# An encoder block's front stage: conditioning, normalization and first projections put in another order

## The chip, the cores and the metric

One core of a Trainium2 chip (trn2). The time is microseconds of device time for one execution of the program; the kernel before was run three times, and the profile is of one execution of its own.

## What is computed

One layer of an encoder, for two sequences of 512 tokens with 1024 channels and one conditioning vector each; all in fp32. Cut to what matters here:

```python
mod = silu(c) @ w_ada + b_ada                       # 1024 -> 6 x 1024
sh1, sc1, gt1, sh2, sc2, gt2 = split(mod, 6)
h = rmsnorm(x, g_attn) * (1 + sc1) + sh1
z = h @ w_in                                        # 1184 columns here, 2048 of gates later
qa, ka, va, cq, ckv, kr, gla, glb = split(z)
# mixer A: windowed attention on rope(rmsnorm(qa)), rope(rmsnorm(ka)), va
# mixer B: rmsnorm(cq) @ w_uq, rmsnorm(ckv) @ w_ukv, norm, rope, dense attention
x = x + gt1 * ((sigmoid(gla) * (oa @ w_o_a) + sigmoid(glb) * (ob @ w_o_b)) @ w_out)
# then an MLP with a depthwise convolution, modulated by sh2, sc2, gt2
```

A projection in fp32 accuracy is three matmuls of fp32r halves (`mm3`: high x high, high x low, low x high), so each weight and each activation is first split into a high part (a cast) and a low part (the residual).

## The kernel before

The front stage, which the change rebuilds, runs in this order (lines are those of the profile):

- **Constants.** Small loads on SP's queue: `colt`, `gcol` twice, `c_in`, `bcol` (L59 to L139). The Silu of c gives `c_s`.
- **Normalization of the first sequence.** `norm(t)` (L243) loads 128 tokens of x, squares them on ACT in two halves (L249), forms 1/rms by a Sqrt and a Newton step on VectorE (`rsqrt`, L83) and scales the tile on VectorE (L254).
- **First loop**, eight turns k (L269). Each loads 1 MB of the weights of sh1 and sc1 (`w_ada`, three buffers, L271), multiplies (64 small matmuls, L281), copies the row (L286), transposes the first sequence's block k of x (L104) and the row (L289), runs the first projection (`project`, 416 columns: cq, ckv, kr) for the block before, completes `mod` and `a1` (L295, L297), and makes the block's h: ACT scales and shifts (L112), VectorE casts (L113) and forms the residual (L114). In turns 3 to 6 stands `norm` of the second sequence's tiles; in turn 7 the rope tables are loaded and multiplied with the gains on VectorE (`tables`, L190; `table`, L171). The projection's weights are split on POOL (`split_pool`, L69 and L72).
- **Second sequence's h**, eight blocks (L301), with the low-rank weights w_uq and w_ukv loaded into the `w_ada` buffers and split by ACT and VectorE in between (`low_rank`, L218, L230, L231).
- **Low-rank stage** (mixer B), `prep_b` (L340) for eight tiles of 128 tokens in three steps that overlap; for the second sequence `z_tile` (L329) makes the tile's projection first. Its results go to DRAM on SP's queue (L403).
- **Mixer A**, two parts of 384 columns: `weights(1)`, `weights(2)` load and split (L201, ACT casts L210, residuals L212 on POOL, some on VectorE in part 2), then eight tiles each of `z_tile` and `prep_a` (L405). Between the tiles stands one step of `ada()` (L141): the conditioning's second half, two parts of eight steps, each a 1 MB load and four matmul groups of 512 columns (L151); after each part VectorE adds the bias (L155), TensorE transposes (L158), VectorE copies to `mod`.

Behind it come the gates' products (L491, weights split on POOL), which fill TensorE during attention, then attention, the output projection and the MLP.

What sets the order: each engine runs its instructions in the order of one list, which a scheduler forms from the program; it may put a later instruction first where an earlier one isn't ready by its own model of times. Instructions marked `keep_in_program_order` stay in place. All DMAs are issued from SP's queue, in order; a store that waits for its data holds the loads behind it. Tiles of a pool share a number of buffers (`bufs`), handed out in program order.

## Time and profile before

| | |
|---|---|
| three runs, median (lowest, highest) | 1456.73 us (1453.19, 1458.41) |
| profiled execution, its own time | 1456.77 us |
| its span, first to last instruction | 1455.0 us |
| granted clock of TensorE, mean | 0.992 |
| DMA, mean over the span | 133 GB/s |

A row of the timeline is a merged group of like instructions. "Idle before" is the time in which the engine did nothing just ahead of the instruction, with what ended it. PE is TensorE, DVE VectorE, ACT ScalarE, POOL GpSimd; SPq is the queue that issues DMAs. In a table by stage the numbers of an engine are busy microseconds and, in brackets, instructions; PEclk is the granted clock of TensorE, 1.00 being full speed; the DMA share is that of 16 engines' time.

### The profile page before, as it was taken

The numbers are of one execution on the slowest core, as the hardware profiler recorded it, in microseconds if no ns is written. First come the engines' busy times: TensorE is split into PE (matmuls) and PEld (weight loads), VectorE is DVE, ScalarE is ACT, GpSimd is POOL, SyncE is SP. The second block draws the span as 40 slices with busy tenths as digits, with TensorE's granted clock in tenths as the row PEclk, the third lists the DMA queues.
The fourth block names the chain that finished last, engine by engine and source line by source line (L and its number), as shares of the span: only waits on it lengthen the run. The fifth ranks groups of instructions, "written<-read, shape, count | busy, mean of one in ns | idle before, by whom it ended". The sixth has DMA issues, their size and how long they took to land.

```text
span 1455.0 us, 20795 instructions
## 1 busy us (share of the span) xinstructions
PE 1391.8 (96%) x7184; PEld 1153.1 (79%) x7184; DVE 1000.3 (69%) x1907; ACT 679.3 (47%) x1385; POOL 596.0 (41%) x592
## 2 busy tenths in 40 slices
PE   5888998999999999999998899999999999999998
PEld 4777776888888888878887767888888888888887
DVE  5788776666678886545479888777777787447433
ACT  3475223666666665422347455555555554212210
POOL 3174023442433442381005755555555545544430
PEclk9999999999999999999999999999999999999999
DMA  8565763322222213655312322222222327646522
GB/s 342 176 216 170 236 239 135 116 88 87 88 87 73 102 64 120 236 176 200 133 39 73 120 74 87 87 82 85 87 85 82 102 73 250 205 148 223 180 87 73
DMA packets 107801, 193.82 MB, mean 133 GB/s; under 512 B 18856, under 2 KB 39592, under 8 KB 104624
## 3 DMA queue, kind: packets, MB, share of 16 engines
q1 hardware_dynamic: 107696, 192.49, 39.8%
q8 instruction: 57, 0.93, 0.3%
q14 instruction: 48, 0.39, 0.1%
HBM read 148.39 MB, written 44.06 MB: 132 GB/s over the span
## 4 chain that ended last, share of the span: by engine, by line
PE 77%; DVE 13%; POOL 3%; ACT 2%; DMA 2%; issue 2%; SPq 0%; ACTq 0%; POOLq 0%; DVEq 0%
PE px L955 13%; PE psg L491 11%; PE py L955 7%; PE psd L79 5%; PE psd L80 5%; PE psd L81 5%; PE pz L955 3%; PE ppt L512 3%; PE ppo L575 2%; PE psx L81 2%; PE psx L80 2%; PE psx L79 2%; PE psz L79 2%; PE psy L81 1%; PE psy L79 1%
## 5 line engine op out<-in xcount | busy, mean ns | idle before, releaser
L955 PE MATMUL px<-t,wt 128*128 128x512 f32 x792 | 191.2, 391 | 7.0 <-ACT tmp_cc L960 6.3
L922 POOL TENSOR_TENSOR wt<-wraw,wt 128x512 fp32r<-128x512 f32 x66 | 92.8, 1410 | 232.2 <-ACT wt L921 232.0
L955 PEld LDWEIGHTS px<-t,wt 128*128 128x128 f32 x792 | 148.0, 188 | 41.1 <-ACT tmp_cc L960 9.5
L491 PE MATMUL psg<-h_hi,wg 128*128 128x512 f32 x512 | 170.2, 397 | 0.0
L506 POOL TENSOR_SCALAR p<-p,l 128x512 f32<-128x512 f32 (+2 forms) x128 | 78.8, 617 | 200.3 <-DVE l L505 125.7
L76 DVE TENSOR_TENSOR wd<-wraw,wd 128x512 fp32r<-128x512 f32 x88 | 93.1, 1098 | 96.4 <-ACT wd L75 96.4
L79 PE MATMUL psd<-wd 128*128 128x512 f32 x352 | 136.9, 389 | 0.0
L80 PE MATMUL psd<-wd 128*128 128x512 f32 x352 | 136.9, 389 | 0.0
L81 PE MATMUL psd<-wd 128*128 128x512 f32 x352 | 136.9, 389 | 0.0
L75 ACT CAST wd<-wraw 128x512 fp32r<-128x512 f32 x88 | 51.3, 620 | 156.1 <-issue 86.9
L491 PEld LDWEIGHTS psg<-h_hi,wg 128*128 128x128 f32 x512 | 95.9, 189 | 18.4 <-POOL wg L69 0.8
L491 PE MATMUL psg<-h_lo,wg 128*128 128x512 f32 x256 | 101.8, 397 | 0.0
L504 ACT ACTIVATE p<-pps,nm 128x512 f32<-128x512 f32 (+2 forms) x128 | 78.2, 611 | 39.3 <-DVE nm L501 31.7
L922 DVE TENSOR_TENSOR wt<-tmp_sf,wt 128x512 fp32r<-128x512 f32 x88 | 82.2, 944 | 12.2 <-ACT wt L921 12.0
L967 DVE SCALAR_TENSOR_TENSOR tmp_u<-tmp_cc,cw,tmp_u 128x511 f32<-128x511 f32 x66 | 64.3, 974 | 37.3 <-ACT tmp_u L966 37.2
L69 POOL TENSOR_SCALAR wd<-wraw 128x512 fp32r<-128x512 f32 x44 | 34.2, 777 | 112.0 <-PE psd L81 63.9
L81 PEld LDWEIGHTS psd<-wd 128*128 128x128 f32 x352 | 66.1, 188 | 13.8
L79 PEld LDWEIGHTS psd<-wd 128*128 128x128 f32 x352 | 66.1, 188 | 13.7
L80 PEld LDWEIGHTS psd<-wd 128*128 128x128 f32 x352 | 66.1, 188 | 13.6
L501 DVE TENSOR_REDUCE nm<-pps 128x1 f32<-128x512 f32 (+2 forms) x128 | 74.7, 584 | 3.1 <-PE pps L81 1.5
L966 ACT ACTIVATE tmp_u<-tmp_cc,cw 128x512 f32<-128x512 f32 x66 | 53.6, 813 | 45.7 <-DMA g_d<-tmp_u 25.6
L72 POOL TENSOR_TENSOR wd<-wraw,wd 128x512 fp32r<-128x512 f32 x44 | 72.7, 1653 | 3.7
(257 smaller groups left out, 3517.8 us busy)
## 6 DMA issues: line engine op xcount, KB each, us to landing
w_ada<-in_w_ada_dram SPq DMA_DIRECT2D x24, 1024.0 KB, 7.1
wraw<-in_w_up_dram SPq DMA_DIRECT2D x96, 256.0 KB, 2.7
wraw<-in_w_down_dram SPq DMA_DIRECT2D x88, 256.0 KB, 3.6
g_d<-tmp_u SPq DMA_DIRECT2D x44, 256.0 KB, 2.4
wraw<-g_d SPq DMA_DIRECT2D x44, 256.0 KB, 2.7
wg_raw<-in_w_g_dram SPq DMA_DIRECT2D x16, 512.0 KB, 3.7
gate_d<-go SPq DMA_DIRECT2D x32, 256.0 KB, 2.0
ldb<-qb_d SPq DMA_DIRECT2D x8, 1024.0 KB, 4.9
```

Of the source, the lines that this page charges most:

```text
L72: G.tensor_sub(lo, raw, hi.bitcast(F32))
L76: V.tensor_sub(lo, raw, hi.bitcast(F32))
L79: PE.matmul(ps, lhsT=lh, rhs=rh, start=first, stop=False)
L80: PE.matmul(ps, lhsT=lh, rhs=rl, start=False, stop=False)
L81: PE.matmul(ps, lhsT=ll, rhs=rh, start=False, stop=last)
L491: PE.matmul(ps, lhsT=w[:, wl, m, k, :], rhs=hl[b][:, k, :], start=k == 0 and n == 0, stop=k == KD - 1 and n == 2)
L501: V.tensor_reduce(nm, ps[:, :n], op=ALU.max, axis=AX.X, negate=True)
L504: A.activation(p[:, :n], ps[:, :n], AF.Exp, bias=nm, accum_out=l)
L506: G.tensor_scalar(out=p[:, :plen], in0=p[:, :plen], scalar1=l, scalar2=1.0, op0=ALU.mult, op1=ALU.mult)
L922: lo_eng.tensor_sub(w[:, 1], raw, w[:, 0].bitcast(F32))
L955: PE.matmul(ps[:, sl], lhsT=w[:, wl, i], rhs=h[:, hl, sl], start=not add and i == 0 and n == 0, stop=i == 3 and n == 2, skip_group_check=add)
L967: V.scalar_tensor_tensor(out=u[:, 1:S], in0=src[:, 0:S - 1], scalar=cw[:, cc, 0:1], in1=u[:, 1:S], op0=ALU.mult, op1=ALU.add)
```

## The change

- The two `gcol` loads move behind the second sequence's h; `colt` and `bcol` behind the four loads of x.
- Normalization: tiles in pairs. One square of 1024 elements a tile (written to `h_lo[1]` or `h_hi[1]`, which are not in use yet), one root for two tiles; tile 3 is scaled on ACT. The second sequence's tiles are loaded in turns 2 to 5 and squared on ACT in the same turns; in turn 5 one root for all four, scaled on ACT. A Sqrt of a constant stands ahead of it all.
- Sixty transposes of the identity on TensorE ahead of the first turn; their result isn't used.
- In the first loop the projection of the block before is cut in two, on both sides of the row's transpose. The second sequence's first block is made in turn 7.
- The rope tables stand after the loop, behind the loads of the first two low-rank weights, and are multiplied on POOL.
- `ada()` loads two steps ahead, from the end of the second sequence's h on. Its steps stand in the low-rank stage: three a tile in the first four tiles, then one a tile; none in mixer A.
- `weights_late` loads the weights of mixer A in two pieces of four blocks into the `w_ada` buffers; part 1 is split at the end of the low-rank stage, part 2 ahead of the last `prep_a` of part 1; residuals go to POOL and VectorE in turn.

```diff
@@ table
-            V.tensor_mul(tc_, tc_, bcast(g, 1, [128, NT, dim]))
+            G.tensor_mul(tc_, tc_, bcast(g, 1, [128, NT, dim]))
...
@@ ada
+            ws = []
+
+            def load():
+                n = len(ws)
+                if n < 2 * KD:
+                    w = zp.tile([128, KD, 4, 64], F32, name="w_ada", bufs=3).rearrange("p a b c -> p (a b c)")
+                    SY.dma_start(w, w_ada[n // KD, n % KD])
+                    ws.append(w)
+
+            load()
+            load()
+            yield
             for part in range(2):
...
                 for k in range(KD):
-                    w = zp.tile([128, KD, 4, 64], F32, name="w_ada", bufs=3).rearrange("p a b c -> p (a b c)")
-                    SY.dma_start(w, w_ada[part, k])
+                    load()
+                    w = ws[part * KD + k]
@@ new
+        def weights_late(part):
+            c0, cw = ZC[part]
+            raws = []
+            for k in range(0, KD, 4):
+                raw = zp.tile([128, KD, 4, 64], F32, name="w_ada", bufs=3).rearrange("p a b c -> p (a b c)")[:, :4 * cw]
+                raw = raw.rearrange("p (k n) -> p k n", k=4)
+                SY.dma_start(raw, w_z[:, k:k + 4, c0:c0 + cw])
+                raws.append(raw)
+
+            def split():
+                tiles = []
+                for k in range(KD):
+                    w, raw = zp.tile([128, 2, ZB], F32R, name="wz", bufs=10), raws[k // 4][:, k % 4]
+                    A.copy(w[:, 0, :cw], raw)
+                    (V if k % 2 else G).tensor_sub(w[:, 1, :cw], raw, w[:, 0, :cw].bitcast(F32))
+                    tiles.append(w)
+                return tiles
+            return split
@@ normalization of the first sequence
+            for t in range(NT):
+                load_x(t)
+            SY.dma_start(colt, cols)
+            SY.dma_start(bcol, b_col)
+            one = wk.tile([128, 1], F32, name="one")
+            V.memset(one, 1.0)
+            tc.keep_in_program_order(A.activation(one, one, AF.Sqrt))
+            for t in range(0, NT, 2):
+                ss = wk.tile([128, 2], F32, name="ss", bufs=2)
+                for j in range(2):
+                    xt = xn[t + j].rearrange("p (a n) -> p a n", a=2)
+                    A.activation(h_lo[1][:, 2 * (t + j):2 * (t + j) + 2, :], xt, AF.Square, accum_out=ss[:, j:j + 1])
+                r = scales(ss)
+                V.tensor_scalar(out=xn[t], in0=xn[t], scalar1=r[:, 0:1], scalar2=None, op0=ALU.mult)
+                if t:
+                    A.activation(xn[t + 1], xn[t + 1], AF.Copy, scale=r[:, 1:2])
+                else:
+                    V.tensor_scalar(out=xn[t + 1], in0=xn[t + 1], scalar1=r[:, 1:2], scalar2=None, op0=ALU.mult)
+
+            idle = pst.tile([128, S], F32, name="pst")
+            for j in range(60):
+                PE.transpose(idle[:, (j % NT) * 128:(j % NT + 1) * 128], ident, ident)
@@ first loop
-                if 3 <= k < 7:
-                    norm(NT + k - 3)
-                if k == 7:
-                    tables()
+                if 2 <= k < 6:
+                    load_x(NT + k - 2)
...
-                xt = transposed(pst, xn[:NT], k, True)
+                xt = transposed(pst, xf[:NT], k, True)
+                if k:
+                    project(k - 1, 0, 2)
                 pt = psa.tile([64, 128], F32, name="psa")
                 tc.keep_in_program_order(PE.transpose(pt, row, ident))
                 if k:
-                    project(k - 1)
+                    project(k - 1, 2, NT)
...
                 modulated(wk, xt, 0, a1, 0, h_hi[0], h_lo[0], k)
-            project(KD - 1)
-            for k in range(KD):
-                split = low_rank(k // 2) if k % 2 == 0 else split
-                modulated(wk, transposed(pst, xn[NT:], k), 1, a1, 0, h_hi[1], h_lo[1], k)
-                if k % 2:
-                    split()
+                if 2 <= k < 6:
+                    t = NT + k - 2
+                    A.activation(h_hi[1][:, 2 * (k - 2):2 * (k - 1), :], xn[t].rearrange("p (a n) -> p a n", a=2), AF.Square,
+                                 accum_out=ss1[:, k - 2:k - 1])
+                if k == 5:
+                    r1 = scales(ss1)
+                    for t in range(NT):
+                        A.activation(xn[NT + t], xn[NT + t], AF.Copy, scale=r1[:, t:t + 1])
+                if k == 7:
+                    second_batch()
+            project(KD - 1, 0, NT)
+            mods = ada()
+            splits = [low_rank(n) for n in range(2)]
+            tables()
+            for k in range(0, KD, 2):
+                if k == 4:
+                    splits += [low_rank(n) for n in range(2, 4)]
+                second_batch()
+                second_batch()
+                splits[k // 2]()
+            next(mods)
+            SY.dma_start(gcol[0:NOPE, 0:1], gains[2 * AD:2 * AD + NOPE].unsqueeze(1))
...
@@ low-rank stage and mixer A
             for t in range(2 * NT + 2):
+                for _ in range(3 if t < NT else 1):
+                    next(mods, None)
+                if t == 2 * NT - 1:
+                    later = weights_late(1)
...
+                if t == 2 * NT:
+                    tiles = later()
...
-            mods = ada()
+            later = weights_late(2)
             for part in range(2):
-                tiles = weights(1 + part)
                 for t in range(2 * NT):
-                    prep_a(t, z_tile(t, tiles, ZC[1 + part][1]), part)
-                    next(mods, None)
-            for _ in mods:
-                pass
+                    zt = z_tile(t, tiles, ZC[1 + part][1])
+                    if not part and t == 2 * NT - 1:
+                        tiles = later()
+                    prep_a(t, zt, part)
```

`scales` is the mean, the epsilon and `rsqrt` for all its columns; `second_batch` is one block of the second sequence's h, as before: four transposes and `modulated`.

## Rows read from the trace of the kernel before

**Rows 1.** The page, part 1: busy time of each engine, share of the span, instructions.
```profile
PE 1391.8 (96%) x7184; PEld 1153.1 (79%) x7184; DVE 1000.3 (69%) x1907; ACT 679.3 (47%) x1385; POOL 596.0 (41%) x592
```

**Rows 2.** Busy time of each engine by stage, the front in five stretches.
```profile
core 0: us, PE busy (x) PEld busy (x) DVE busy (x) ACT busy (x) POOL busy (x), PEclk, DMA share, GB/s
0.00:14.50 14.50, 0.00 (x0) 0.01 (x1) 3.75 (x22) 8.37 (x22) 0.96 (x7) 1.00 0.71 259
14.50:60.95 46.45, 38.69 (x655) 33.02 (x656) 30.97 (x102) 14.32 (x33) 14.01 (x16) 0.96 0.71 255
60.95:73.20 12.25, 11.10 (x65) 9.24 (x63) 11.71 (x23) 8.67 (x15) 2.62 (x2) 1.00 0.78 274
73.20:146.00 72.80, 63.44 (x330) 53.58 (x329) 61.87 (x179) 46.12 (x127) 44.52 (x79) 0.98 0.58 193
146.00:226.00 80.00, 73.50 (x429) 57.99 (x428) 62.03 (x212) 19.27 (x51) 18.94 (x19) 0.97 0.71 231
```

**Rows 3.** The same for the stretch in which the first loop loads.
```profile
14.00:40.00 26.00, 21.35 (x395) 18.30 (x395) 18.21 (x56) 7.84 (x20) 10.83 (x12) 1.00 1.02 400
```

**Rows 4.** The timeline of the first loop: start, duration, engine, line, operation, [idle before].
```profile
3.55 1.85 SPq L245 DMA_DIRECT2D xt<-in_x_dram  x4
14.52 1.94 PE L281 MATMUL pa<-w_ada,c_s 128*32 128x64 f32 x64 [14.52 <-DMA w_ada<-in_w_ada_dram]
17.84 1.52 DVE L254 TENSOR_SCALAR xt<-xt,r 128x1024 f32<-128x1024 f32 x1
29.76 1.10 PE L281 MATMUL pa<-w_ada,c_s 128*32 128x64 f32 x64
33.75 1.10 PE L281 MATMUL pa<-w_ada,c_s 128*32 128x64 f32 x64
33.87 2.71 POOL L72 TENSOR_TENSOR wz<-wz_raw,wz 128x416 fp32r<-128x416 f32 x2
34.91 0.33 SPq L271 DMA_DIRECT2D w_ada<-in_w_ada_dram  x1
54.70 1.10 PE L281 MATMUL pa<-w_ada,c_s 128*32 128x64 f32 x64
```

**Rows 5.** The chain of waits in the fifth turn: start, duration, what.
```profile
33.44 1.01 DVE xt L254
35.69 1.43 DVE h_lo L114
```

**Rows 6.** VectorE's groups by line, 14.5 to 73.2 us: busy us, mean ns, idle before.
```profile
L114 DVE TENSOR_TENSOR h_lo<-tmp,h_hi 128x512 fp32r<-128x512 f32 x16 | 12.5, 792 | 0.3
L113 DVE CAST h_hi<-tmp 128x512 fp32r<-128x512 f32 x16 | 7.5, 476 | 5.2 <-ACT tmp L112 5.2
L231 DVE TENSOR_TENSOR ukv<-w_ada,ukv 128x512 fp32r<-128x512 f32 x2 | 2.2, 1087 | 0.0
L231 DVE TENSOR_TENSOR uq<-w_ada,uq 128x768 fp32r<-128x768 f32 x2 | 1.9, 950 | 0.0
```

**Rows 7.** Durations of products on VectorE and POOL, ns min/median/max.
```profile
L177 DVE TENSOR_TENSOR tca<-tca,g_tab x2: 420/423/426, 60.4 to 62.8; 128x256 f32<-128x256 f32 x2
L324 POOL TENSOR_TENSOR t1b<-qf,tcb x8: 725/862/1510, 81.5 to 138.5; 128x256 f32<-128x256 f32 x8
L212 DVE TENSOR_TENSOR wz<-wz_raw,wz x4: 547/554/809, 116.3 to 175.8; 128x384 fp32r<-128x384 f32 x4
```

**Rows 8.** TensorE's conditioning matmuls, 73.2 to 226 us: busy us, mean ns, idle before.
```profile
L151 PE MATMUL psa<-w_ada,c_s 128*32 128x512 f32 x128 | 18.1, 604 | 0.0
```

**Rows 9.** DMA issues of the front: count, KB each, median us to landing.
```profile
w_ada<-in_w_ada_dram SPq DMA_DIRECT2D x24, 1024.0 KB, 7.1
```

**Rows 10.** The timeline where the front stage ends.
```profile
206.59 0.17 DVE L95 TENSOR_SCALAR rs<-rs 128x6 f32<-128x6 f32 x1
213.17 1.25 DVE L95 TENSOR_SCALAR rs<-rs 128x6 f32<-128x6 f32 x1
224.76 1.12 PE L158 MATMUL psa<-ident,br 128*128 128x128 f32 x4 [6.13 <-DVE br L155]
```

More of the change, by code (lines that the diff above doesn't have):

```diff
@@ L58, in encoder_block @@
     colt = const.tile([128, 16], F32, name="colt")
-    SY.dma_start(colt, cols)
     mod = const.tile([128, 48, NB], F32, name="mod")
@@ L64, in encoder_block @@
     V.memset(gcol, 1.0)
-    SY.dma_start(gcol[0:NOPE, 0:1], gains[2 * AD:2 * AD + NOPE].unsqueeze(1))
-    SY.dma_start(gcol[0:NOPE, 1:2], gains[2 * AD + BQK:2 * AD + BQK + NOPE].unsqueeze(1))
     def split_pool(hi, lo, raw, in_order=False):
@@ L241, in encoder_block, with load_x @@
             xn = [None] * (2 * NT)
-            def norm(t):
+            def load_x(t):
                 xt = wk.tile([128, D], F32, name="xt", bufs=2 * NT)
                 SY.dma_start(xt, x[t * 128:(t + 1) * 128, :])
-                ss = wk.tile([128, 2], F32, name="ss", bufs=4)
-                for q in range(2):
-                    junk = wk.tile([128, S], F32, name="tmp", bufs=2)
-                    A.activation(junk, xt[:, q * S:(q + 1) * S], AF.Square, accum_out=ss[:, q:q + 1])
-                r = wk.tile([128, 1], F32, name="r", bufs=4)
-                V.tensor_add(r, ss[:, 0:1], ss[:, 1:2])
-                mean_eps(r, r, D)
-                rsqrt(wk, r, 1)
-                V.tensor_scalar(out=xt, in0=xt, scalar1=r, scalar2=None, op0=ALU.mult)
-                xn[t] = lambda k, xt=xt: xt[:, k * 128:(k + 1) * 128]
@@ L257, in encoder_block, with scales, part_of @@
-            for t in range(NT):
-                norm(t)
+                xn[t] = xt
+            def scales(ss):
+                n = ss.shape[1]
+                r = wk.tile([128, 4], F32, name="r", bufs=3)[:, :n]
+                mean_eps(r, ss, D)
+                rsqrt(wk, r, n)
+                return r
+            def part_of(t):
+                return lambda k: xn[t][:, k * 128:(k + 1) * 128]
+            xf = [part_of(t) for t in range(2 * NT)]
+            for t in range(NT):
+                load_x(t)
@@ L261, in encoder_block, with project @@
             cw = ZC[0][1]
-            def project(k):
-                for t in range(NT):
+            def project(k, t0, t1):
+                for t in range(t0, t1):
                     sl = slice(t * 128, (t + 1) * 128)
@@ L267, in project, with second_batch @@
                         k == 0, k == KD - 1)
+            ss1 = wk.tile([128, NT], F32, name="ss1")
+            r1 = None
+            second = iter(range(KD))
+            def second_batch():
+                k = next(second, None)
+                if k is not None:
+                    modulated(wk, transposed(pst, xf[NT:], k), 1, a1, 0, h_hi[1], h_lo[1], k)
             for k in range(KD):
@@ L299, in encoder_block @@
                 modulated(wk, xt, 0, a1, 0, h_hi[0], h_lo[0], k)
-            project(KD - 1)
-            for k in range(KD):
-                split = low_rank(k // 2) if k % 2 == 0 else split
-                modulated(wk, transposed(pst, xn[NT:], k), 1, a1, 0, h_hi[1], h_lo[1], k)
-                if k % 2:
-                    split()
+                if 2 <= k < 6:
[20 more added lines that the diff above has]
+            SY.dma_start(gcol[0:NOPE, 0:1], gains[2 * AD:2 * AD + NOPE].unsqueeze(1))
+            SY.dma_start(gcol[0:NOPE, 1:2], gains[2 * AD + BQK:2 * AD + BQK + NOPE].unsqueeze(1))
             zfirst = []
```

5 lines of the change are left out of this document (2 added, 3 removed).

## The prediction

> **What bounds the kernel now.** The page comes first: over the span TensorE is busy 96% of the time, VectorE 69% [rows 1], so a gain must come from stretches where TensorE is held up. The table by stage shows where those are [rows 2]: nothing runs on TensorE for 14.5 us; in the next 46.45 us (first half of the conditioning, first projection) it is busy 38.69; then 11.10 of 12.25, 63.44 of 72.8 and 73.50 of 80. The column beside it names the partner: from 60.95 to 146 VectorE is busy 11.71 of 12.25 and 61.87 of 72.8. After 226 us the kernel is attention and MLP, which the change doesn't touch. Lost time on TensorE between 14.5 and 226 us is 24.8 us (211.5 less 186.7), and 14.5 stand before it.
>
> In the first loop the DMA queue is the first limit: 400 GB/s from 14 to 40 us at a share of 1.02 [rows 3]. The last of its eight weights is issued at 34.91 us [rows 4]; with the median landing of 7.1 us [rows 9] it is there at 42.0, but TensorE reads it only at 54.70 [rows 4]. An undisturbed turn takes 4.0 us (29.76 to 33.75); the last three take 21 together, 9 more than three such turns. The chain of waits shows by what [rows 5]: the second sequence's normalization runs on VectorE in the middle of the chain, and the residual of h after it takes 1.43 us, beside a split on POOL [rows 4].
>
> At the end of the front stage the page hides a wait [rows 10]: TensorE stands 6.13 us until VectorE has added the conditioning's bias. VectorE is slow there, since the gates' weights are being split on POOL: a 128x6 product takes 1.25 us where it took 0.17 a little earlier.
>
> The profiled execution took 1456.77 us (span 1455.0), the median of the three runs is 1456.73; I sum against 1456.77. A measurement of this kernel can tell about 0.3% (4.4 us) from no change.
>
> **Part by part.** *Start.* Five small loads stand ahead of x, which is issued at 3.55 us [rows 4]: about 0.6 us an issue, an estimate. Two (the gains of q and k) move far back, two go behind x. So x starts some 2 us earlier and the weights some 1.2. The squares become one 1024-wide instruction in place of two halves, and the Sqrt table is loaded before x is there. The last tile of x was scaled at 19.36 us [rows 4]; with two chains for four tiles I get about 15. The first turn's 64 matmuls took 1.94 us against 1.10 later, the pace of 1.2 against 2.4 GHz, after an engine that had done nothing; sixty filler transposes run in that empty time and save 0.8 us in each of the first two turns. They can cost nothing before the first weights (14.52 us), unless they outlast them. None of this counts by itself: weights on the DMA queue decide the loop, so I book only the 1.2 us of their start.
>
> *First loop.* Its stream is 8 x 1.05 MB of weights, 8 x 0.52 MB of x and 4 x 0.43 MB of the first projection, 14.3 MB, or 35.7 us at 400 GB/s. The last weight lands at about 40.8. Normalization of the second sequence leaves VectorE (ACT squares and scales, one root for four tiles). The two halves of the projection around the row's transpose hide the row's copy. Turns of 4.0 us from about 15 us also reach the eighth at 43. Bounds: 40.8 if DMA alone decides, 50 if half of the 9 us stays and POOL's splits still stretch VectorE; I take 43, for the turns undisturbed by normalization did run at 4.0 [rows 4]. Behind it the last projection still needs h of the eighth block and ends some 7.5 us later (6.25 before), near 50.5 in place of 60.95: **-10.4 us**.
>
> The Trainium skill, page "DMA: Bandwidth & Descriptors", section "Where 436 GB/s comes from", holds that HBM to SBUF is bound at about 358 GB/s for a core. By that the stream would take 39.9 us, and the loop would end 4 us later (time 1443); the trace disagrees, with 400 GB/s in rows 3.
>
> *Second sequence's h.* VectorE bounds it: eight casts of 0.48 and eight residuals of 0.79 (means that hold the stretched ones), and the low-rank splits of 2.2 and 1.9 us together [rows 6]. One of the eight moves into the loop; seven and the splits are 13.0 us from 48.6 on, and end at 61.6, where they ended at 73.2: **-11 us in all**, 0.6 more than the loop gave. The tables' twelve products leave VectorE (0.42 us the widest) for POOL, where one of this width took 0.73 to 1.51 [rows 7], so 5 to 10 us in all; POOL is idle then, and only the half for mixer B has to be ready when the low-rank preparation starts. The cover gone, up to 5 us. Their loads now stand on SP's queue behind the first low-rank weights, which before were issued behind them.
>
> *Conditioning's second half* (128 instructions, 18.1 us, [rows 8]) moves from 146 us and later into the low-rank stage: twelve steps over its first four tiles, the other four and the two closings after. There TensorE has 9.4 us free [rows 2], and what it did with that stage, the later projection, it does afterwards. It is work moved, not removed: the gain is in idle time that gets filled. The price is the queue: the stage carries 193 GB/s at a share of 0.58, so 14.0 MB took 42 us of it; 13.6 MB more (13 steps; 3 were loaded ahead already) are 34 us at 400. That is 76 in 72.8, full, and in the first four tiles over full. A store of q, k or v that waits for VectorE on SP's queue holds the next weight behind it, and a late weight holds TensorE's queue with the low-rank matmuls in it, and through them VectorE. Bounds: -9 (all idle filled) to +12 (twelve steps paced by the queue: 12.6 MB and half of the 34 us of other traffic are 48 us, against 36 for four tiles). I take **0**, as the idle filled and the lag are of one size.
>
> *Later projections' weights.* Two loads of 0.79 MB into the conditioning's buffers in place of four small ones, for each half. Eight residuals go half to VectorE, four more than before, 0.55 each [rows 7]: 2.2 us, hidden in 18 us that VectorE has free from 146 on [rows 2]; 2.2 if that cover is gone.
>
> *End of the stage.* With the bias done long before, the 6.13 us go, and with them some 1.5 us in which the first gate matmuls run at half pace after that wait: **-7.6 us**. The tail of VectorE's last tile stays as slow as it is, but TensorE has the gates to do in it, if their weights come as early as the stage ends.
>
> Sum: -11 + 0 - 7.6 = -18.6; 1456.8 - 18.6 = 1438.2, and I say **1439**.
>
> **Rivals.** *Front only* (0.20): the late gain is lost in the low-rank stage, where VectorE was the bound and stays so (61.87 of 72.8 us): only the 11 us arrive, 1446. For it speaks VectorE's share there, against it that TensorE's lost 6.13 us are in no low-rank tile. *POOL blocks VectorE* (0.07): beside a POOL split (33.87 us, [rows 4]) a residual took 1.43 us [rows 5], the mean being 0.79 [rows 6], and in the hand-over 0.17 became 1.25 [rows 10]; the tables' products, now on POOL while the second sequence's h is made, cost VectorE 5 us: 1444. The Trainium skill, "SBUF — State Buffer", "Who interferes with whom", makes it a lock: the later of a POOL and a two-input VectorE instruction waits for the whole of the other; by that rule the rival is certain, and the trace agrees for the rows named. *Everything fills* (0.09): loop at 40.8 and 9 us of idle time gone too, 1427. *Nothing arrives* (0.08): the gates' weights stand behind the last rows of mixer A on SP's queue and are split on POOL; if they come no earlier than now, TensorE waits for them instead of for the bias, and the front's 11 us are lost in the same wait: 1455. It is also the time if the instructions are ordered such that the change doesn't do what it says and the second half stays where it was. *Slower* (0.08): the weights of the conditioning come one at a time. Place: the first four low-rank tiles; a step then takes a landing, 7.1 us [rows 9], in place of 2.6 at full rate. Twelve are 85 us, where four tiles took 36. It decides from the point where more than half the steps lose their prefetch: seven such and five at 2.6 are 63 us, +27, more than the 18.6 gained: 1465. For it speaks that weights and waiting stores share one queue, against it that TensorE never waited for these weights where they stand now, three buffers ahead [rows 8].
>
> **How the numbers follow.** The forecast has 0.48 (its own range 1431 to 1446), front only 0.20, POOL 0.07, everything fills 0.09: faster by over 0.3% together 0.84. Nothing arrives is within 0.3%: 0.08. Slower: 0.08. The range is 1427 to 1453: its lower end is the full filling with both bounds, its upper one the front gain cut to 4 us by a loop that ends at 50 with nothing won later. It leaves out the last two cases, 0.16.
>
> **What would show it.** Right: the eighth group of 64 conditioning matmuls near 43 us in place of 54.70; the last residual of h near 62; matmuls of the second half between 60 and 130 us; no wait of their transposes for the bias at the end; the first gate matmuls near 200. Wrong: TensorE waiting for w_ada in the low-rank stage (slower), a low-rank stage longer than 73 us with VectorE as full as now (front only), POOL's tables beside stretched residuals (POOL), TensorE idle until the gates' first split (nothing arrives). A time above 1453 or under 1427 makes the sum wrong as a whole.

## The result and the profile after

The kernel after took 1465.94 us (median of five runs, 1463.91 to 1469.67), the kernel before 1454.60 (five runs); the ratio of the means is 1.0074, 95% interval [1.0051, 1.0098]. It is slower; the forecast was 1439, and the time lies above the range.

The page alone doesn't show where the time went: TensorE's busy time grew by 17.0 us, of which 9.4 are the sixty transposes, and VectorE's fell by 9.2. What [rows 1] showed for before reads, after,

```profile
PE 1408.8 (96%) x7244; PEld 1168.4 (80%) x7244; DVE 991.1 (68%) x1857; ACT 681.9 (47%) x1370; POOL 594.3 (41%) x600
```

So the table by stage again, cut where the stages of the kernel after begin (it answers [rows 2]): start, first loop, second sequence's h, low-rank stage, mixer A.

```profile
0.00:11.64 11.64, 9.41 (x60) 9.20 (x61) 2.57 (x11) 7.61 (x14) 0.96 (x7) 1.00 0.83 309
11.64:47.20 35.56, 29.97 (x619) 24.51 (x619) 15.67 (x52) 13.83 (x21) 14.05 (x16) 0.95 0.83 327
47.20:67.50 20.30, 18.54 (x119) 15.49 (x108) 14.85 (x28) 12.56 (x21) 7.04 (x13) 1.00 0.52 145
67.50:162.00 94.50, 81.58 (x434) 58.31 (x433) 62.04 (x194) 46.14 (x129) 42.09 (x77) 0.93 0.81 285
162.00:228.00 66.00, 57.30 (x306) 55.60 (x305) 58.97 (x193) 17.86 (x49) 19.50 (x19) 0.95 0.34 101
```

Read it beside [rows 2]. The low-rank stage begins 5.7 us earlier (67.5 against 73.2), but takes 94.5 us in place of 72.8, with VectorE as busy as before (62.04 against 61.87). TensorE stands 12.9 us there, where before it stood 9.4, and runs part of it at less than full clock. Part of the 21.7 us is work that changed place: the conditioning's second half took 4.24 us of TensorE's time in the low-rank stage of before (24 of its 128 matmuls) and 17.60 in that of the kernel after. Mixer A, without the conditioning, is shorter, but TensorE loses 8.7 of 66 us in it, where it had lost 6.5 of 80. The windows of these matmuls alone, before and then after:

```profile
73.20:146.00 72.80, 4.24 (x24) 0.60 (x24) 0.98 0.58 193
67.50:162.00 94.50, 17.60 (x128) 2.62 (x128) 0.93 0.81 285
```

The timeline of the kernel after shows where (first loop, the second sequence's h, SP's queue in the low-rank stage, POOL in mixer A):

```profile
19.24 1.10 PE L337 MATMUL pa<-w_ada,c_s 128*32 128x64 f32 x64
21.70 0.59 DVE L110 CAST h_hi<-tmp 128x512 fp32r<-128x512 f32 x1 [2.96 <-ACT tmp L109]
21.98 2.72 POOL L69 TENSOR_TENSOR wz<-wz_raw,wz 128x416 fp32r<-128x416 f32 x2
22.34 1.43 DVE L111 TENSOR_TENSOR h_lo<-tmp,h_hi 128x512 fp32r<-128x512 f32 x1
27.24 1.20 PE L337 MATMUL pa<-w_ada,c_s 128*32 128x64 f32 x64
...
46.30 1.10 PE L337 MATMUL pa<-w_ada,c_s 128*32 128x64 f32 x64
...
56.77 0.43 DVE L110 CAST h_hi<-tmp 128x512 fp32r<-128x512 f32 x1 [1.93 <-ACT tmp L109]
57.23 1.21 DVE L111 TENSOR_TENSOR h_lo<-tmp,h_hi 128x512 fp32r<-128x512 f32 x1
...
66.96 0.68 DVE L258 TENSOR_TENSOR ukv<-w_ada,ukv 128x512 fp32r<-128x512 f32 x1
...
63.53 27.77 SPq L144 DMA_DIRECT2D w_ada<-in_w_ada_dram  x10
95.34 0.59 SPq L172 DMA_DIRECT2D gt_d<-br  x2
...
97.39 0.60 SPq L478 DMA_DIRECT2D qb_d<-qf  x1
...
170.02 1.46 POOL L66 TENSOR_SCALAR wg<-wg_raw 128x512 fp32r<-128x512 f32 x2 [10.97 <-DVE rs L89]
```

SP's queue issues ten loads of `w_ada`, each when a buffer comes free, then a store that waits for the conditioning's first bias, and only at 97.39 us, one more load behind, the first store of q, k, v. In before four of these loads stood ahead of that store, and it left at 83.3 us, 10 us into the stage; here it leaves 30 us into it. The waits of SP's queue from 60 to 162 us say for what it stood, first the loads' buffers, then the stores' data:

```profile
SPq L144 <- PE psa L158: 21.2, 10, 3.2
SPq L478 <- DVE kf L474: 17.2, 3, 8.2
SPq L478 <- DVE qf L473: 10.2, 3, 5.7
```

q, k and v have two buffers each. So the third tile's copy of q waits until the first tile's store has landed, and the fourth's for the second's. In the timeline of ScalarE, the second and third copies of before, and then the first four of the kernel after, with the copies of z (`zo`) that stand ahead of the third:

```profile
87.10 0.80 ACT L380 COPY qf<-ppq 128x768 f32<-128x768 f32 x1 [0.60 <-PE ppq L81]
94.11 0.80 ACT L380 COPY qf<-ppq 128x768 f32<-128x768 f32 x1
```

```profile
75.64 0.80 ACT L455 COPY qf<-ppq 128x768 f32<-128x768 f32 x1 [2.04 <-PE ppq L78]
82.86 0.80 ACT L455 COPY qf<-ppq 128x768 f32<-128x768 f32 x1 [0.78 <-PE ppq L78]
...
96.41 0.51 ACT L412 COPY zo<-psz 128x416 f32<-128x416 f32 x1 [2.52 <-PE psz L78]
103.31 0.51 ACT L412 COPY zo<-psz 128x416 f32<-128x416 f32 x1 [6.39 <-PE psz L78]
106.17 0.80 ACT L455 COPY qf<-ppq 128x768 f32<-128x768 f32 x1 [2.35 <-DMA qb_d<-qf]
116.28 0.80 ACT L455 COPY qf<-ppq 128x768 f32<-128x768 f32 x1 [0.46 <-DMA qb_d<-qf]
```

Seven us lie between the first two, as in before, and 23 between the second and the third. The waits for the store itself are short (2.35 and 0.46 us), because in ScalarE's list other work was put ahead of the third copy; ScalarE stands 8.9 us for two copies of z there. In the chain of waits the fourth reads

```profile
104.67 11.53 DMA qb_d<-qf
...
116.28 0.81 ACT qf L455
```

The store lands in 11.53 us there, while the DMA engines are full (windows of the kernel after):

```profile
100.00:110.00 10.00, 7.21 (x43) 4.77 (x42) 1.58 (x2) 3.65 (x6) 2.33 (x4) 1.00 1.03 370
110.00:120.00 10.00, 7.04 (x38) 3.34 (x37) 6.62 (x23) 4.93 (x14) 4.97 (x9) 0.83 1.05 389
...
140.00:150.00 10.00, 7.97 (x33) 6.71 (x33) 6.95 (x13) 7.40 (x16) 6.56 (x8) 0.82 0.72 225
```

From 100 to 110 us VectorE works 1.58 us of 10. Behind these ten us, in which TensorE stood for 2.8, its granted clock falls to 0.83, a mixture of 2.4 and 1.2 GHz, and stays at 0.82 to 0.84 until 150 us. Before shows 0.83 too, but only from 110 to 120 us, and e7 shows 1.00 in all of this stretch, though TensorE stands about as long there. So the clock costs here once more; why it falls in one kernel and not in the other, these runs don't show.

### The profile page after: what moved, and what is told of

Its sections match the earlier page's. It is cut to its first block, busy times and chain, and to the rows that moved or that the text cites. A ratio compares the mean times of both kernels' runs of the same rounds, so it can differ in the third digit from the quotient of the medians.

```text
span 1464.1 us, 20839 instructions
## 1 busy us (share of the span) xinstructions
PE 1408.8 (96%) x7244; PEld 1168.4 (80%) x7244; DVE 991.1 (68%) x1857; ACT 681.9 (47%) x1370; POOL 594.3 (41%) x600
## 4 chain that ended last, share of the span: by engine, by line
PE 77%; DVE 12%; DMA 4%; ACT 3%; POOL 3%; issue 2%; SPq 0%; ACTq 0%; DVEq 0%; POOLq 0%
PE px L1035 14%; PE psg L571 9%; PE py L1035 7%; PE psd L77 5%; PE psd L78 5%; PE psd L76 5%; PE pz L1035 3%; PE ppt L592 3%; PE ppo L655 2%; PE psx L76 2%; PE psx L77 2%; PE psx L78 2%; PE psy L78 2%; PE psy L76 2%; PE psy L77 2%
## 5 line engine op out<-in xcount | busy, mean ns | idle before, releaser
L1002 DVE TENSOR_TENSOR wt<-tmp_sf,wt 128x512 fp32r<-128x512 f32 x88 | 85.2, 977 | 12.1 <-ACT wt L1001 11.7
L1047 DVE SCALAR_TENSOR_TENSOR tmp_u<-tmp_cc,cw,tmp_u 128x511 f32<-128x511 f32 x66 | 63.3, 958 | 34.6 <-ACT tmp_u L1046 34.6
L76 PEld LDWEIGHTS psd<-wd 128*128 128x128 f32 x352 | 66.1, 188 | 13.8
L77 PEld LDWEIGHTS psd<-wd 128*128 128x128 f32 x352 | 66.1, 188 | 13.7
L78 PEld LDWEIGHTS psd<-wd 128*128 128x128 f32 x352 | 66.1, 188 | 13.6
L1049 DVE SCALAR_TENSOR_TENSOR tmp_u<-tmp_cc,cw,tmp_u 128x511 f32<-128x511 f32 x66 | 75.0, 1136 | 1.4
```

The costliest lines, as they stand in the source:

```text
L76: PE.matmul(ps, lhsT=lh, rhs=rh, start=first, stop=False)
L77: PE.matmul(ps, lhsT=lh, rhs=rl, start=False, stop=False)
L78: PE.matmul(ps, lhsT=ll, rhs=rh, start=False, stop=last)
L1002: lo_eng.tensor_sub(w[:, 1], raw, w[:, 0].bitcast(F32))
L1047: V.scalar_tensor_tensor(out=u[:, 1:S], in0=src[:, 0:S - 1], scalar=cw[:, cc, 0:1], in1=u[:, 1:S], op0=ALU.mult, op1=ALU.add)
L1049: V.scalar_tensor_tensor(out=u[:, 0:S - 1], in0=src[:, 1:S], scalar=cw[:, cc, 2:3], in1=u[:, 0:S - 1], op0=ALU.mult, op1=ALU.add)
```

## The experiments

The profiles' landmarks in microseconds: start of the last residual of h, issue of the last q, k, v store, issue of mixer A's last store, first product of the attention's output projection. Ratios are of the means, against before in the same session, with 95% intervals. e1 to e4, e5 to e8, e9 to e12, e13 to e16 and e17 with e18 are one session each; across sessions only ratios are compared, and two of them are told apart where their intervals don't meet. Below, the length of a stage "by the table" is the difference of two neighbouring landmarks.

| kernel | last h residual | last q, k, v store | last mixer A store | output projection | ratio to before |
|---|---|---|---|---|---|
| before | 72.5 | 145.4 | 228.7 | 584.0 | |
| e9 before again | 69.5 | 142.2 | 225.9 | 583.8 | one run |
| after | 66.4 | 161.2 | 234.1 | 589.2 | 1.0074 [1.0051, 1.0098] |
| e1 front only | 64.9 | 137.6 | 220.4 | 577.8 | 0.9972 [0.9953, 0.9990] |
| e2 move only | 70.9 | 164.2 | 237.6 | 592.5 | 1.0052 [1.0033, 1.0070] |
| e3 early weights | 65.0 | 157.5 | 233.5 | 589.0 | 1.0054 [1.0036, 1.0072] |
| e4 two a tile | 66.3 | 151.1 | 223.2 | 578.4 | 0.9984 [0.9969, 0.9999] |
| e5 stores on ACT | 65.8 | 158.9 | 231.8 | 586.5 | 1.0043 [1.0021, 1.0064] |
| e6 three buffers | 65.9 | 159.3 | 231.9 | 587.1 | 1.0026 [1.0008, 1.0044] |
| e7 from third tile | 65.0 | 147.5 | 220.8 | 576.8 | 0.9966 [0.9949, 0.9982] |
| e8 spread | 65.5 | 139.1 | 233.9 | 588.5 | 1.0059 [1.0042, 1.0077] |
| e10 gates in order | 66.2 | 148.6 | 210.3 | 576.1 | 0.9973 [0.9955, 0.9990] |
| e11 bias early | 66.8 | 141.1 | 222.7 | 579.8 | 0.9979 [0.9966, 0.9992] |
| e12 both | 66.0 | 139.5 | 213.3 | 579.2 | 0.9990 [0.9976, 1.0004] |
| e13 gates ahead | 65.8 | 148.4 | 213.8 | 570.2 | 0.9922 [0.9899, 0.9945] |
| e14 with ACT | 66.1 | 150.2 | 214.4 | 570.0 | 0.9906 [0.9888, 0.9923] |
| e15 on e11 | 66.7 | 140.7 | 215.6 | 572.9 | 0.9927 [0.9904, 0.9949] |
| e16 on after | 66.3 | 161.3 | 229.7 | 586.7 | 1.0018 [1.0005, 1.0032] |
| e17 old front | 70.1 | 154.1 | 218.4 | 573.8 | 0.9929 [0.9916, 0.9942] |
| e18 no fillers | 64.9 | 148.0 | 212.2 | 567.5 | 0.9889 [0.9869, 0.9908] |

### Which part costs the time: e1, e2, e3

e1 puts conditioning's second half and mixer A's weights back; e2 is the old front with the new places of both; e3 takes only `weights_late` back.

> The kernel after, with conditioning's second half back between the tiles of mixer A and mixer A's weights loaded and split as before: only the front (normalization, loop, tables) is rebuilt. Theory Q (the low-rank stage loses its time because ten 1 MB loads of w_ada, each waiting for a buffer, stand ahead of the q, k, v stores on SP's queue): the stage is back at 72 to 78 us in place of 94.5, the start of the stage stays near 67.5 us, and the time is 1444 to 1451. Rival F (the rebuilt front is itself to blame, by the tables on POOL or a clock that stays low): stage above 85 us, time 1456 or more.

> The kernel before, with conditioning's second half in the low-rank stage, loaded two steps ahead, and mixer A's weights loaded late into its buffers; the front is the old one. Theory Q: the stage is 90 to 97 us as in the kernel after, and the time is 1468 to 1478, slower than after by the 6 to 8 us of the front. Rival F: the stage is near 73 to 80 us and the time 1446 to 1457.

> The kernel after, with mixer A's weights loaded in four small pieces and split as before, conditioning's second half still in the low-rank stage. Theory Q: q, k, v stores still wait behind w_ada loads, the stage still takes 88 to 95 us, of which later projections may fill a little, so 1455 to 1463. Rival W (the loss comes from mixer A's weights arriving only at 133 us, so that nothing is there to fill TensorE's gaps): 1438 to 1450. A time of 1464 or more says that the late weights cost nothing.

The front alone is faster by 0.28%, 4 us; its low-rank stage takes 72.7 us by the table, as Q said; the time, 1455.83, is above Q's range, in a session in which before took 1459.25. The move alone is slower by 0.52%, with a stage of 93.3 us; but by the ratios it isn't slower than the kernel after, where Q had 6 to 8 us. So the loss sits in the move. The two parts don't add up to the whole (+0.24% against +0.74%), and e3, which has the new front and the moved conditioning, is no faster than e2 in the same session: beside the moved loads these runs show no gain of the front. Early weights leave the stage at 92.5 us and the time within the interval of the kernel after; W falls, and what the late weights cost or give is below what these runs tell.

### Queue or bytes: e4 to e7

```diff
 e4
-                for _ in range(3 if t < NT else 1):
+                for _ in range(2):
 e5
-                    SY.dma_start(rows[:, :, c0:c0 + w], ...
+                    A.dma_start(rows[:, :, c0:c0 + w], ...
 e6
-                qf = wk.tile([128, BH, BQK], F32, name="qf", bufs=2)
+                qf = wk.tile([128, BH, BQK], F32, name="qf", bufs=3)
...
 e7, behind the tile's stages in place of ahead of them
-                for _ in range(3 if t < NT else 1):
+                for _ in range(0 if t < 2 else 3 if t < 7 else 1):
```

> The kernel after, with two steps of conditioning a tile in the low-rank stage in place of three in the first four tiles and one behind. About eight loads in place of ten stand ahead of the first store. Theory Q: the first store is issued some 5 to 8 us earlier than at 97 us, the stage takes 82 to 90 us, the time is 1453 to 1461. Rival D (the DMA queue is simply full, whatever the order, with the same 16 MB of w_ada in the same tiles): stage 92 us or more, time 1463 to 1468.

> The kernel after, with the q, k, v stores of the low-rank stage issued from ScalarE's queue instead of SP's; the w_ada loads stay on SP's, in the same number and order. Theory Q (order on one queue): the first store leaves as soon as its data is there, near 80 us in place of 97.4, tile 3 doesn't wait for it, the stage takes 76 to 88 us and the time is 1448 to 1458. Rival D (the DMA engines are full, so a store's data wait behind the loads' whichever queue issues it): landings of 8 to 12 us, stage 90 us or more, time 1462 to 1468. A store on ScalarE's queue waits there for VectorE and POOL, which may cost some microseconds in either case.

> The kernel after, with three buffers in place of two for qf and kf (vf keeps two); the order on SP's queue is the same, ten loads ahead of the first store. Theory Q, second half (the late store reaches the engines through the two buffers of qf and kf): the third tile's copy of q no longer waits for the first store, TensorE's matmuls of the third tile run before 116 us, the conditioning steps behind them too, so the stage is 4 to 9 us shorter than 94.5 and the time is 1456 to 1462. Rival L (the coupling isn't those buffers but the loads' own pace, 1 MB at a time): stage and time as after, 1463 to 1468.

> The kernel after, with the conditioning's steps beginning in the third tile and behind that tile's instructions in program order: three a tile in tiles 2 to 6, then one. Two loads, in place of ten, stand ahead of the first store. Theory Q: the first store is issued near 80 us, the stage takes 80 to 90 us, 1450 to 1458, equal to two a tile or up to 4 us better. Rival D (the same bytes in fewer tiles): stage above 90 us, time 1460 to 1468.

Fewer loads ahead of the first store bring back most: e4 issues that store at 84.6 us and is 0.90 points under the kernel after, e7 (at 75.8 us) 1.08 points, some 16 us. The expectation counts two loads ahead of that store in e7; its trace has four, as in before, against eight in e4 and ten and one in the kernel after. Both times lie in Q's ranges, and the stages take 84.8 and 82.5 us by the table, so the bytes alone (D) aren't the limit. With the third buffer (e6) the first store leaves at 97.4 us as before, but the third tile's copy of q no longer waits for it; the jump, 16 us, moves to the fourth tile, without a wait of ScalarE just ahead of it (timeline of ScalarE in e6):

```profile
82.36 0.80 ACT L455 COPY qf<-ppq 128x768 f32<-128x768 f32 x1 [0.78 <-PE ppq L78]
91.18 0.80 ACT L455 COPY qf<-ppq 128x768 f32<-128x768 f32 x1 [1.91 <-PE ppq L78]
107.27 0.81 ACT L455 COPY qf<-ppq 128x768 f32<-128x768 f32 x1
```

So the two buffers are a way by which the late store reaches the engines: one more moves the jump back by a tile and doesn't remove it. How much of the loss goes through them stays open. The ratio falls by 0.48 points, with intervals that just don't meet, but by the table the stage is shortened by 1.4 us only, where Q had 4 to 9, and the output projection begins 2.1 us sooner.

e5 corrects the theory. The first stores leave ScalarE's queue from 78.3 us on (the first of q at 83.7, 14 us earlier), yet the stage still takes 93.1 us, and the time, 1464.43 us, is as rival D said and not clear of the kernel after's (the intervals overlap). ScalarE's waits from 66 to 165 us:

```profile
ACT qf L455 <- DMA qb_d<-qf: 11.8, 2, 6.8
ACT qf L455 <- DVE cn L428: 7.0, 2, 3.8
...
ACT qf L455 <- DMA qb_d<-kf: 5.0, 1, 5.0
```

The stores land in 6.8 us in the median (12.0 at most), against 3.7 in the kernel after and 3.3 in before, while with the stores out of their way the loads fill the DMA engines (375 GB/s from 80 to 90 us). The Trainium skill, "DMA: Bandwidth & Descriptors", section "Issuing engines are not separate DMA queues", says that DMAs run on the same 16 engines whichever engine issues them; e5 agrees. So both theories hold a part: the order on SP's queue delays the first stores by 14 us and more, and the burst itself delays what has been issued. Later and fewer loads cure both, another queue only the first. Part of e5's loss is also its own: ScalarE waits for VectorE's products there, and TensorE 6.1 us for `w_ada`. So e5 doesn't tell what the queue's order alone costs.

### Why the end gave nothing: e8, e10 to e12

e8 is the new front with one conditioning step a tile, the rest in mixer A, and the old weights. e10 is e7 with the gates' first two splits marked to stay behind mixer A's on POOL; e11 is e1 with conditioning begun four steps sooner; e12 is both edits on e1.

> The rebuilt front, one conditioning step a tile in the low-rank stage, the remaining steps between the tiles of mixer A, and mixer A's weights loaded and split as before. Theory Q: five to six loads ahead of the first store and a third of the bytes less in the stage, so the stage takes 76 to 84 us, the bias is added early enough that its wait at the end is gone, and the time is 1446 to 1454, the best of those so far. Rival V (VectorE bounds the low-rank stage, and nothing is won by filling TensorE there): as with the front alone, 0.996 to 0.999 of before.

> The variant whose conditioning begins in the third tile, with the first two splits of the gates' weights on POOL kept in program order, so behind the splits of mixer A's second part. Theory P (with the loads of conditioning out of mixer A's way, the gates' weights arrive 40 us early, and their splits on POOL stand ahead of the second part's splits and stretch VectorE): TensorE's gap between 165 and 200 us (8 to 11 us in the variants with conditioning moved) closes by 4 us or more, and the time is 1443 to 1449. Rival V (mixer A is bound by VectorE once the conditioning's matmuls no longer fill TensorE between its tiles, whoever splits what): the gap moves later, the time stays within 2 us of the variant without this edit, 0.995 to 0.998 of before.

> Only the front rebuilt, mixer A's weights as before, conditioning's steps one a tile as before but begun in the seventh tile of the low-rank stage, so four steps sooner. It tests the last term of the prediction alone: the bias is added some 18 us before the end of the front stage, so the wait of 6.7 us at the end goes. If that term was right, the time is 6 to 8 us less than with the front alone: 0.991 to 0.994 of before. Rival N (TensorE then waits for mixer A's last tiles or the gates' weights instead): 0.995 to 0.998.

> The same with the first two splits of the gates' weights kept in program order on POOL. Theory P: if the gates' splits move forward there too and stretch VectorE in mixer A, this is 2 to 5 us faster than without; if they come behind mixer A's splits anyway, the same within 2 us.

e8 missed by far, with 1467.41 us. Its low-rank stage takes 73.6 us, less than the 76 to 84 that Q said, and then mixer A loses more than was won, in two places (windows of e8):

```profile
130.00:150.00 20.00, 9.92 (x49) 6.58 (x48) 6.18 (x14) 5.21 (x10) 6.83 (x9) 0.74 0.84 283
190.00:210.00 20.00, 13.69 (x67) 13.29 (x68) 14.69 (x36) 4.36 (x10) 6.95 (x7) 0.74 0.30 90
```

In the first TensorE waits for mixer A's split weights (6.7 us in one wait) and for `w_ada` (3.3). In the second it waits for the second part's residual on POOL (4.9 us in one wait), which stands behind the gates' splits. A hole of the same kind is in the kernel after and in e7 (8.7 and 6.7 of the 35 us from 165 to 200), where the waits end with VectorE's residuals and ScalarE's copies of z more than with POOL. With the conditioning's loads gone from mixer A, SP's queue reaches the gates' weights early, and POOL splits them from 170.02 us on, where in before they came at 210.17. Beside them VectorE's small products stretch, in mixer A of the kernel after (groups of VectorE, 170 to 200 us):

```profile
L86 DVE TENSOR_TENSOR rsq_u<-rs,rsq_y 128x4 f32<-128x4 f32 x6 | 3.5, 581 | 0.1
...
L88 DVE TENSOR_SCALAR rsq_u<-rsq_u 128x4 f32<-128x4 f32 x6 | 2.8, 467 | 0.2
```

That is the stretching that [rows 10] had shown at the end of before, now in the middle of a stage where VectorE is busy 32.87 of 35 us. The windows from 165 to 200 us of the kernel after, then of e10:

```profile
165.00:200.00 35.00, 26.30 (x130) 24.60 (x129) 32.87 (x97) 8.96 (x26) 19.50 (x19) 0.90 0.42 123
```

```profile
165.00:200.00 35.00, 35.00 (x201) 35.00 (x200) 33.19 (x125) 11.98 (x31) 3.34 (x3) 1.00 0.19 54
```

e10 closes the hole wholly and issues mixer A's last store at 210.3 us, 10.5 earlier than e7. So the gap is as P said, and V's reason falls: without the conditioning's matmuls TensorE is busy all the time, with VectorE at 33.19 of 35 us. But the time is e7's, as V had it, for another reason: kept in order, the gates' splits come behind the mask's first instructions, which wait for mixer A's last store, and TensorE waits for them (timeline of e10):

```profile
213.93 0.79 PE L571 MATMUL psg<-h_hi,wg 128*128 128x512 f32 x1 [8.47 <-POOL wg L66]
```

e11 is the same lesson on e1, and e12 that of e10: its splits begin at 216.4 us, and nothing is won. In e11 the bias wait (6.7 us in e1) is gone, and the time, 0.9979, is as with the front alone and as rival N said: the gates' splits begin at 191.9 us in place of 201.7, and mixer A's tail is stretched by them (timeline of VectorE in e11):

```profile
191.09 0.17 DVE L88 TENSOR_SCALAR rsq_u<-rsq_u 128x6 f32<-128x6 f32 x1
...
199.15 1.25 DVE L86 TENSOR_TENSOR rsq_u<-rs,rsq_y 128x6 f32<-128x6 f32 x1
```

### The splits in their place: e13 to e16

In all four the gates' first weight is split right behind mixer A's second part and ahead of the mask, the next weight behind the mask; in e14 to e16 its high halves are cast on ScalarE, which leaves POOL four residuals.

```diff
+        gate = gates()
+        next(gate)
         mask = wk.tile([128, 2, 128], F32, name="mask")
...
+                        if f == 0:
+                            A.copy(w[:, 0, m, k:k + 4], raw[:, k:k + 4])
+                            tc.keep_in_program_order(G.tensor_sub(w[:, 1, m, k:k + 4], ...))
+                        else:
+                            split_pool(..., f < 2)
```

> Conditioning begun in the third tile; the gates' first weights are split on POOL right behind the splits of mixer A's second part and ahead of the mask, whose memory waits for the front's last store (with the mask ahead of them TensorE waited 8.5 us for the first such split). Theory P (the gates' splits cost either TensorE a wait or VectorE its pace, by where they stand on POOL): gap between 165 and 200 us mostly closed, first gate matmul with no wait for POOL, but prep_a's tail stretched by some microseconds: 1445 to 1451, 0.992 to 0.996 of before. Rival V: 0.996 to 0.999, as with both earlier placements.

> The same with the high halves of the gates' first weight cast on ScalarE, which is busy a third of the time there; POOL does four residuals in place of eight instructions. Theory P: less POOL time beside VectorE, so 1 to 4 us better than with all on POOL, 1443 to 1449, 0.990 to 0.995 of before. Rival V: no difference between the two, both 0.996 to 0.999.

> Only the front rebuilt, conditioning four steps sooner but still mostly between the tiles of mixer A, with the same treatment of the gates' first weight. Theory P: the end-of-stage gain that was missed with the bias alone comes now: 0.991 to 0.995 of before. Rival V: 0.997 to 0.999, as without it.

> The kernel after, three steps a tile from the first tile, with the same treatment of the gates' first weight. Theory Q and P together: the low-rank stage stays at 94 us, the gap in mixer A (some 8 us) shrinks by 4 to 6: 1459 to 1462, 1.001 to 1.004 of before. If the queue's stall were the whole loss, it would stay at 1.006 to 1.008.

P holds in all four. e13 is 0.44 points under e7, e14 0.60 (the two overlap, so the casts' share isn't told apart), e16 0.56 under the kernel after, in each case with intervals that don't meet. The window of e14, beside the two above:

```profile
165.00:200.00 35.00, 34.16 (x194) 33.66 (x194) 33.88 (x112) 10.96 (x30) 9.59 (x7) 1.00 0.27 76
```

e15 is 0.52 points under e11, 7.6 us, but that is what the gates' edit gives and not the last term of the prediction, though the number is the same. That term is nearer to e15 against e1, early bias and gates' edit together: 0.45 points, 6.6 us. How much of it is the early bias isn't shown, since the gates' edit wasn't run on e1 alone. So something of that size was there to be had, but with an edit that the change doesn't contain.

### The front: e9, e17, e18

> The kernel before, unchanged, for a profile from the same chip as the other experiments. If the stretch behind the front (first attention output to the end) takes 866 us as in the profile of before, the 3 to 5 us that all variants lose there belong to the change; if it takes 869 to 871 as in the variants, they are the chip's and nothing was lost behind the front.

> The best variant so far (conditioning begun in the third tile, gates' first weight ahead of the mask with its high halves on ScalarE), with the normalization, first loop and tables of the kernel before. It measures the first term of the prediction (11 us) where nothing behind it takes it back. If that term was right, 1454 to 1458, 10 to 12 us more than the best variant's 0.9906; the traces so far (last h residual 3 to 7 us earlier than in two profiles of before) say 4 to 7 us more: 0.993 to 0.996.

> The best variant without the sixty transposes of the identity ahead of the first turn. The prediction booked nothing for them, since the weights on the DMA queue decide the loop: the first two turns' conditioning matmuls go back to about 1.9 us, the time stays within 2 us of the best variant: 0.989 to 0.992. If TensorE's pace decides the loop, it is 2 us or more slower.

e9 took 1460.16 us; from the first output projection to the last matmul of the last projection it took 869.7 us, the first profile of before 866.2, the kernel after 870.0. So nothing is lost behind the front, and what the profile of after shows there (3.8 us) isn't the change's. Up to that point the profiles of after and of before differ by 5.2 to 5.4 us; the ratio says some 11 with an interval from 7. The rest I can't place: runs of one kernel spread by several microseconds.

With e14's other edits the old front (e17) costs 0.23 points, 3.4 us, against e14 (the intervals overlap), and 0.40 points, 5.8 us, against e18 in the same session. So the rebuilt front gives 3 to 6 us, not 11. e18, without the fillers, is the fastest of all, 0.9889. Its interval overlaps e14's, so that the fillers cost time isn't shown; that TensorE's pace decides the loop is not borne out. In the loop they seem to cost: the eighth turn, in e14 and then in e18:

```profile
46.10 1.10 PE L337 MATMUL pa<-w_ada,c_s 128*32 128x64 f32 x64
```

```profile
43.74 1.10 PE L334 MATMUL pa<-w_ada,c_s 128*32 128x64 f32 x64
```

In the fifteen profiles with fillers that turn begins at 44.96 to 46.84 us. But the lead is gone at the last residual of h, where e18 is level with e1. The fillers do bring the first two turns to 1.10 us of conditioning matmuls (1.94 and 1.72 without). But the turn that begins at 19.24 us in the kernel after then takes 8.0 us: a POOL split meets the cast and the residual of h (21.70 to 22.34 us above), where in e18 the turn that begins at 20.59 takes 3.98, the residual 0.69. From 24 to 28 us TensorE's granted clock is 0.57 in the kernel after, and 1.00 in e14 and e18. That this meeting is the reason wasn't tried.

## Why the prediction was wrong

- **Conditioning's second half, priced at 0** with "I take **0**, as the idle filled and the lag are of one size". This is the step that failed most. By the table the low-rank stage took 21.9 us longer than before and mixer A 10.4 us less: 11.5 us lost over both, where the sum had 0 and -7.6. By e4 and e7 the burst of loads is worth 13 to 16 us of the time. The queue was seen, but in one direction only: "A store of q, k or v that waits for VectorE on SP's queue holds the next weight behind it". Such waits are there (27.4 us for `kf` and `qf` above), but they cost TensorE no wait for a weight. What cost was the other direction: the loads held the stores on the queue and in the DMA engines, and through two buffers ScalarE, VectorE and TensorE. The upper bound of +12 was worked out from bytes; it left out the two-buffer coupling and the clock behind it. It was also too low by its own working: it counts 34 us of other traffic, which is the time of the new loads, where the other traffic took 42 us, and with that it is +16. And the conditioning didn't stand wholly "from 146 us and later": 24 of its 128 matmuls ran in the low-rank stage already.
- **The "Slower" rival**, at 0.08, gave 1465 and the right place, with another mechanism, so that its number is luck: in the low-rank stage TensorE's list of waits has no wait for `w_ada` at all. Its weights were on time, at the stores' expense.
- **End of the stage, -7.6 us.** Its condition stood in the text: "if their weights come as early as the stage ends". They came too early: their splits begin 40 us sooner than in before. The bias wait went and TensorE lost 8.7 us in mixer A, where it had lost 6.5 with the bias wait. The prediction priced the conditioning's matmuls as work moved; it didn't ask what their loads had held back on SP's queue.
- **Start and first loop, -10.4 us.** "I take 43": 46.30, and 43.74 without the fillers, which "can cost nothing before the first weights" and perhaps did, though they ended ahead of them. The direction was right; worth 3 to 6 us.
- **Second sequence's h, "-11 us in all".** VectorE's share was priced well: the last seven blocks and the splits took 10.9 us (56.77 to 67.64 above), where the sum had 13.0. But they began at 56.77 in place of 48.6, for which no row is given, and VectorE stood 5.5 us of the stretch for ScalarE's scaling. The last residual was put at 61.6 and began at 66.4. (From 73.2 to 61.6 are 11.6 us, not 11.)
- **Later projections' weights, 0 to 2.2 us**: nothing measurable (e3), in agreement.
- **"Front only"** is what e1 gives by itself, with 4 us in place of its 11. **"POOL"**: beside the tables one residual took 1.21 us, but from 47.2 to 67.5 us the ten residuals took 0.75 in the mean and the casts 0.48, so about 1 us more than undisturbed (0.69 and 0.43), not 5. The prediction speaks of two-input VectorE instructions and says that the trace agrees for the rows named; the residual has two inputs, but the product of [rows 10] is a TENSOR_SCALAR with one.

Of the signs named in advance, three of the wrong ones showed: a low-rank stage longer than 73 us (though with a VectorE that stood, not one as full as before), stretched residuals beside POOL's tables (one of them), and a time above 1453. So did three of the right ones, at least in part (eighth turn, second half's matmuls from 69 us on, no bias wait), which is why single signs weren't enough. The first gate matmuls came at 229.1, not near 200.

## What to carry to other kernels

When loads move to an earlier stage, write down the order of the issuing queue there: each load that waits for a buffer stands ahead of that stage's stores, and the stores' buffers can carry the delay to every engine. Ask also what the moved loads had kept back where they stood; what arrives sooner is processed sooner, and may take an engine's slack in a stage that has none. Begin a prefetch no earlier than the stage's own stores allow (e4, e7), and look at every stage that it passes through: e8 spread it over two stages, kept the low-rank stage at 73.6 us, and lost more than that in mixer A. From the kernel after to e18 little changes but when and where work is issued, besides the sixty transposes, and 1.85 points lie between them.

## What the runs showed of the hardware

- The stores of q, k and v (256 to 384 KB) landed in 3.3 us in the median of before (2.9 to 5.4); beside a full burst of loads single ones took 11.53 and up to 12.0 us, from SP's queue (the kernel after) as from ScalarE's (e5).
- VectorE's 128x4 products took 0.47 and 0.58 us in the mean (L88, L86) beside POOL's splits, 1.25 single ones, against 0.15 to 0.17 undisturbed, the one-input product of L88 among them; POOL's own residuals of 128x512 took 1.38 in the mean there and 1.29 from 230 us on. In this stretch it is VectorE's small products that pay most.
- Sixty transposes ahead of the first weights brought the first two turns' matmuls from 1.94 and 1.72 us to 1.10, and the eighth turn began 2.4 us later (46.10 in e14 against 43.74 in e18, one profile each).
- From 10 to 36 us the first loop of the kernel after moved 415 GB/s, more than the 400 of [rows 3].
